# Feed-forward blocks in two halves, a third piece split by a transfer, and a first product in two matmuls

## The chip, the cores and the metric

The kernel runs on one core of one Trainium2 chip. Its time is the time of one execution on the device in microseconds (us). The kernel before took 2339.63 us, the median of three runs (2338.91 to 2342.20). The engines are called as in the profile: PE (matmuls; PEld its weight loads), DVE (VectorE), ACT (ScalarE), POOL (GpSimd) and SP, which here only issues transfers.

## The reference

One decoder layer on 256 tokens of 2048 features, all in float32. It runs a feed-forward part (FFN), a token mixer with two branches (sparse attention and a gated recurrence), and a second FFN, each followed by a layer norm:

```python
def swiglu(h, w_in, w_out):
    a, b = jnp.split(h @ w_in, 2, axis=-1)
    return (jax.nn.silu(a) * b) @ w_out

h = layer_norm(DN_ALPHA * h + 0.5 * swiglu(h, ffn1_w_in, ffn1_w_out), ln1_g, ln1_b)
...                       # projections, attention, recurrence, gates
h = layer_norm(DN_ALPHA * h + merged @ w_out, ln2_g, ln2_b)
h = layer_norm(DN_ALPHA * h + 0.5 * swiglu(h, ffn2_w_in, ffn2_w_out), ln3_g, ln3_b)
```

The inner width of each FFN is 5632: `w_in` is 2048 x 11264, `w_out` 5632 x 2048. Both FFNs run the same code, `ffn` (L1124), and the change lies there.

## The kernel before, in words

**Three products for one.** A float32 product is made of three matmuls in the format fp32r: every operand is split into a high part h (the value copied to fp32r by ACT) and a low part l (the value minus h, by DVE). `three` (L742) multiplies high by high, high by low and low by high into the same sums. The activations stand still in the array (128 x 128) and the weights stream past: 512 columns in `tokens` (L747), 256 in the forms below. So every weight has to be read from memory, copied by ACT (L275) and subtracted by DVE (L276).

**Blocks and chunks.** `w_in` of an FFN is cut into 22 blocks (`NBK`) of 256 columns of a and the 256 of b that belong to them. A block is four chunks of 512 rows. A chunk can go plainly, or by the scheme of seven products instead of eight (Strassen's in Winograd's form): the 2 x 2 quarters of the weights are added up on DVE (`operand`, L222: lines 230, 234, 237), and the seven products, of 256 columns each, are grouped into four *forms*: `p1q3`, `p2`, `q5p7` and `q4p6`. `p2` has one product, the other forms two, and each product is two units of three matmuls: 42 matmuls of 256 columns in a chunk. In blocks 6 to 21 (`FOUR`) all four chunks go by forms; these are the long blocks. The products add up in two banks `mm` (c) and two banks `bp` (e). `gate` (L1125) joins them at the block's end: ACT copies one quarter (L1132), DVE adds (L1133, L1134, L1135, L1139), ACT applies silu (L1140), DVE multiplies (L1145); some pieces later PE transposes the result (L1151) and it is split (L878, L879) into tiles g.

**Fills.** The second product, g @ `w_out`, is put among the blocks: `"o"` in a plan is a *piece* of `w_out`, 1024 columns wide in the tile and worth 12 matmuls of 512 columns. The blocks are grouped (`SEGS`: 2, then five times 4). While the blocks of one group run, the g of the group before is multiplied: each long block takes four pieces (k = 0, 2, 4, 6) for one quarter of the output columns; the sums then leave by ACT (L1174) and an adding transfer (L1175). With g as the group's number, blocks 6 to 9 work on g = 1 and blocks 10 to 21 on g = 2, 3 and 4.

**The plan.** `block_plan(FAST, 4, 3)` writes the order of a long block: three pieces, eight forms (two chunks), one piece, eight forms. PE, SP and POOL run in the order in which the program is written; ACT and DVE run in an order that a planner fixes before the run from its own costs.

**The supply of weights.** `Weights` walks one list of all pieces and forms. `unit` (L282) hands the next columns to PE; when it goes on to a new piece (`cur`), it loads up to `cur + AHEAD + LOADS` = 8 ahead (`load_to`, L216, on SP) and splits up to 4 ahead (`split_to`). Chunks of 1 MB are loaded into tiles `rf` (three of them in an FFN), pieces of 0.5 MB into `raw` (four), and split parts stand in five tiles `hl`.

**Pieces by transfer.** Some pieces take another way (`far`, `far_to`, L167): ACT writes minus the copy into a tile `wd` (L182), POOL issues a transfer that adds the piece from memory to it (L183), which gives l without DVE, and ACT writes h (L185). That is done `EARLY` = 12 pieces ahead, all four copies and both transfers at once; the raw tile is loaded four pieces before. The pieces k = 2 and k = 6 go this way, in g = 0 only for two quarters of the output: 34 pieces in an FFN.

Of the kernel before, what the change touches and what calls it, by code (L numbers as in the profile page):

```python
# [16 lines left out]
S = 256  # L17
# [43 lines left out]
HL_PITCH = 2112  # L61
BEGINS = (48, 16, 0)
AHEAD = 4
EARLY = 12
LOADS = 4
FORMS = ("p1q3", "p2", "q5p7", "q4p6")
PIECE = 1024
FAST = (0, 1, 2, 3)
# [31 lines left out]
FOUR = tuple(range(6, 22))  # L100


def layer_plans():
    three = (1, 2, 3)
    plans = [block_plan((), 0)] * 2
    plans += [block_plan((1, 3), 2, 0)] + [block_plan(three, 2, 2, late=False)] * 3
    for n in range(6, NBK):
        plans.append(block_plan(FAST if n in FOUR else three, 4, 3))
    return plans


# [26 lines left out]
class Weights:  # L138
# [8 lines left out]
    def __init__(self, nc, pool, pieces, on_piece):  # L147
        self.nc, self.pool, self.on_piece = nc, pool, on_piece
        self.fast_pool = self.third = None
        self.chunks = 0  # L150
        self.wide = None
        self.pieces = pieces
        self.raw = {}
        self.sums = {}
        self.hl = {}
        self.loaded = 0
        self.split = 0
        self.cur = -1
        self.limit = None
        self.cap = len(pieces)  # L160
        self.off = 0
        self.far = []
        self.apart = ()
        self.far_raw = {}
        self.far_loaded = self.far_split = 0

    def far_to(self, i):  # L167


        nc = self.nc  # L170
        while self.far_loaded < len(self.far) and self.far[self.far_loaded] <= i + LOADS:
            k = self.far[self.far_loaded]
            ap = self.pieces[k][0]
            t = self.far_raw[k] = self.pool.tile([P, PIECE], F32, name=f"raw{k}", tag="raw", bufs=RAW_BUFS)
            nc.sync.dma_start(t, ap)
            self.far_loaded += 1
        while self.far_split < len(self.far) and self.far[self.far_split] <= i:
            k = self.far[self.far_split]
            ap, t = self.pieces[k][0], self.far_raw.pop(k)
            h, l = ([self.wide() for _ in range(2)] for _ in range(2))  # L180
            for c in range(2):
                nc.scalar.activation(l[c], t[:, c * 512:(c + 1) * 512], AF.Copy, scale=-1.0)  # L182
                nc.gpsimd.dma_start(l[c], ap[:, c * 512:(c + 1) * 512], accum_op=OP.add)  # L183
            for c in range(2):
                nc.scalar.activation(h[c], t[:, c * 512:(c + 1) * 512], AF.Copy)  # L185
            self.hl[k] = (h, l)
            self.far_split += 1

    def key(self, i):
        ap, form = self.pieces[i]  # L190
# [91 lines left out]
    def unit(self, n):  # L282
        if self.cur < 0 or self.off == self.size(self.cur):
            self.hl.pop(self.cur, None)
            self.cur += 1
            self.off = 0
            self.far_to(self.cur + EARLY)
            self.load_to(self.cur + AHEAD + LOADS)
            self.split_to(self.limit or min(self.cur + AHEAD, self.cap))
            self.on_piece(self.size(self.cur) * (1 if self.pieces[self.cur][1] else 2))  # L290
        h, l = self.hl[self.cur]
        o = self.off
        self.off += n
        assert self.off <= self.size(self.cur)
        if self.cur in self.apart or self.cur in self.far:
            return h[o // 512], l[o // 512]
        return h[:, o:o + n], l[:, o:o + n]
# [70 lines left out]
def tile_layer(ctx, tc, x_fm, x_tm, pos, f1a, f1o, wA, wki, wB, wG, lru, wab, wrb, wo, f2a, f2o,  # L368
# [33 lines left out]

    bg = Background()

    pieces, far, apart = [], [], set()

    def keep_apart(n):
        apart.update(range(len(pieces) - n, len(pieces)))
# [6 lines left out]
    def block_pieces(ap, plan, fills=None, fo=None):  # L415
        chunk = {}
        for f, k in plan:
# [3 lines left out]
                plain([next(fills)])  # L421
            elif f == "o":
                g, nb, k = next(fills)
                if k in (2, 6) and (g or nb >= 2):
                    far.append(len(pieces))
                k += 2 * SEGS[g][0]
                pieces.append((fo[nb][:, k * 512:k * 512 + PIECE], None))
            else:
                if k not in chunk:
                    chunk[k] = ap[:, k * 2048:(k + 1) * 2048]  # L430
                pieces.append((chunk[k], f))
# [52 lines left out]
    keep_apart(WIDE)  # L484

    W = Weights(nc, pool, pieces, bg.paced)
    W.far, W.apart = far, apart
    W.across = {v.tensor.name for v in (wki, wB, lru)}
    W.wide = lambda: U("wd", F32R)
    W.fast_pool = ctx.enter_context(tc.tile_pool(name="f1", bufs=1))  # L490
# [251 lines left out]
    def three(ps, xh, xl, w, start, stop):  # L742
        T.matmul(ps, xh, w[0], start=start, stop=False)  # L743
        T.matmul(ps, xh, w[1], start=False, stop=False)  # L744
        T.matmul(ps, xl, w[0], start=False, stop=stop)  # L745

    def tokens(ps, x, t, w, start, stop):  # L747
        three(ps, x[:, 0, t * P:(t + 1) * P], x[:, 1, t * P:(t + 1) * P], w, start, stop)

    def eager(hs, ps):  # L750
# [28 lines left out]
    def blockF(x, forms, plan, fill):  # L779
# [14 lines left out]
        for i, (form, k) in enumerate(plan):  # L794
# [25 lines left out]

            def run(ps, ops, start, stop):
                for r in range(2):
                    three(ps, *ops[r], W.unit(S), start and r == 0, stop and r == 1)

            if form == "p1q3":
                run(p1, xop(0, 0), start[2], stop[2])
# [297 lines left out]
    def ffn(x, forms, ln):  # L1124
# [51 lines left out]

        for s, (b0, b1) in enumerate(SEGS):
            for n in range(b0, b1):
                c, e = blockF(x, forms, PLANS[n], fill)
                task = gate(c, e, g[s], 2 * (n - b0), LAG_T[n == NBK - 1], ("c", 0) in PLANS[n])  # L1180
                with tc.high_priority():
                    next(task)
                bg.add("gate", task)
        def back():
            for nb in range(4):
                for t in range(2):
# [509 lines left out]
```

## Time and profile before

| | before |
|---|---|
| median of three runs | 2339.63 us |
| profiled execution, its own time | 2340.27 us |
| its span | 2338.4 us |
| busy PE / DVE / ACT / POOL | 2312.5 / 2201.5 / 1560.0 / 263.4 us |
| one long block (of 32) | 31.4 us |
| moved by DMA | 546.97 MB, 234 GB/s on the mean |

A row of a timeline is: start, duration, engine, line, operation, the tile written and the tiles read, the shape, how many; in brackets the idle time before it and who ended it. `mm` and `bp` are banks of sums, `hl` split weights, `rf` and `raw` weights as loaded, `wd` the parts of a piece by transfer, `ws` the sums of quarters, `sh`/`sl` and `xs`/`hs` split activations, `z` the gate's tile, `g` its result. Matmuls are pipelined: a row's duration runs past the next one's start, so the distance of the starts is the pace. In the same way a DVE row's duration runs a little past the start of the next. In rows by stretch, the numbers are the length, then for each engine its busy time and its count of instructions, the granted clock as a share of full speed, the DMA engines' busy share, and GB/s.

### The profile page before, as it was taken

To read this page: it belongs to the slowest core of one execution; us is meant where nothing else is said; L and a number is where in the kernel's file an instruction comes from. 1 tells how busy PE (TensorE), PEld (TensorE's weight loads), DVE (VectorE), ACT (ScalarE), POOL (GpSimd) and SP (SyncE) were. 2 spreads that over 40 slices of the span, in tenths; PEclk is the share of its full clock that TensorE was granted. 3 is DMA by queue.
4 is the path that set the end of the run, shared out by engine and by line. 5 is a ranking of instruction groups with operands and counts; after the bars stand their busy time and mean duration, and the time that the engine had idled before them with its cause. 6 is when DMAs were issued, how large, how long until landed. Compare 5 with 4: busy or idle time off the path is not lost.

```text
span 2338.4 us, 40427 instructions
## 1 busy us (share of the span) xinstructions
PE 2312.5 (99%) x15430; PEld 2109.4 (90%) x15430; DVE 2201.5 (94%) x3196; ACT 1560.0 (67%) x2273; POOL 263.4 (11%) x368
## 2 busy tenths in 40 slices
PE   9999999999999999999999999999999999999998
PEld 7899999999988999888899998888889999999997
DVE  7999999999999999979887888998999999999997
ACT  7667777777757656556557785555667777777763
POOL 1101111111110000000100001100111111111111
PEclk9999999999999999999999999999999999999999
DMA  9878988888876556554675658655788888888875
GB/s 336 251 238 240 261 250 251 250 256 250 230 244 209 192 187 216 185 189 154 244 239 193 200 182 326 239 198 195 242 275 232 253 255 252 243 252 267 244 221 215
DMA packets 142178, 546.97 MB, mean 234 GB/s; under 512 B 16640, under 2 KB 17280, under 8 KB 117536
## 3 DMA queue, kind: packets, MB, share of 16 engines
q1 hardware_dynamic: 100800, 455.00, 55.1%
q0 software_dynamic: 41040, 89.27, 18.4%
q8 instruction: 120, 1.97, 0.3%
q14 instruction: 74, 0.61, 0.1%
q10 hardware_dynamic: 144, 0.13, 0.0%
HBM read 507.10 MB, written 37.22 MB: 233 GB/s over the span
## 4 chain that ended last, share of the span: by engine, by line
PE 66%; DVE 23%; issue 5%; DMA 3%; ACT 2%; POOL 0%; SPq 0%; ACTq 0%; DVEq 0%; POOLq 0%
PE mm L743 13%; PE mm L745 13%; PE mm L744 13%; DVE hl L276 13%; PE bp L744 5%; PE bp L745 5%; PE bp L743 4%; PE mm L1390 3%; PE mm L1389 3%; PE mm L1391 3%; DVE ws L230 2%; DVE rf L237 2%; DVE rf L234 2%; ACT hl L275 2%; DMA raw<-f1o 1%
## 5 line engine op out<-in xcount | busy, mean ns | idle before, releaser
L275 ACT ACTIVATE hl<-rf 128x1024 fp32r<-128x1024 f32 x573 | 511.3, 912 | 232.9 <-DVE rf L237 119.7
L276 DVE TENSOR_TENSOR hl<-rf,hl 128x1024 fp32r<-128x1024 f32 x573 | 596.9, 1047 | 8.2 <-ACT hl L275 3.8
L276 DVE TENSOR_TENSOR hl<-raw,hl 128x1024 fp32r<-128x1024 f32 (+3 forms) x402 | 474.2, 1196 | 62.2 <-ACT hl L275 61.4
L275 ACT ACTIVATE hl<-raw 128x1024 fp32r<-128x1024 f32 (+3 forms) x402 | 408.4, 1035 | 179.4 <-PE mm L745 82.8
L744 PE MATMUL bp<-hl,sh 128*128 128x256 f32 x1146 | 323.6, 282 | 10.1 <-DVE hl L276 10.1
L743 PE MATMUL bp<-hl,sh 128*128 128x256 f32 x1146 | 320.9, 280 | 0.0
L745 PE MATMUL bp<-hl,sl 128*128 128x256 f32 x1146 | 320.2, 279 | 0.0
L743 PE MATMUL mm<-hl,hs 128*128 128x512 f32 (+1 forms) x800 | 274.5, 343 | 1.6 <-DVE z L1139 0.7
L275 ACT ACTIVATE hl<-ws 128x1024 fp32r<-128x1024 f32 x191 | 202.0, 1058 | 102.7 <-DVE ws L230 71.5
L744 PE MATMUL mm<-hl,hs 128*128 128x512 f32 (+1 forms) x800 | 268.3, 335 | 0.0
L745 PE MATMUL mm<-hl,hs 128*128 128x512 f32 (+1 forms) x800 | 267.9, 335 | 0.1
L230 DVE TENSOR_TENSOR ws<-rf 128x1024 f32<-128x1024 f32 x191 | 233.8, 1224 | 5.4 <-DMA rf<-wrb 1.3
L276 DVE TENSOR_TENSOR hl<-ws,hl 128x1024 fp32r<-128x1024 f32 x191 | 234.2, 1226 | 1.8 <-ACT hl L275 1.7
L744 PEld LDWEIGHTS bp<-hl,sh 128*128 128x128 f32 x1146 | 215.4, 188 | 17.5 <-DVE hl L276 16.3
L745 PEld LDWEIGHTS bp<-hl,sl 128*128 128x128 f32 x1146 | 217.7, 190 | 0.0
L743 PEld LDWEIGHTS bp<-hl,sh 128*128 128x128 f32 x1146 | 215.4, 188 | 1.3
L1389 PE MATMUL mm<-hs,hl 128*128 128x256 f32 x640 | 178.3, 279 | 0.0
L1391 PE MATMUL mm<-hs,hl 128*128 128x256 f32 x640 | 177.8, 278 | 0.0
L1390 PE MATMUL mm<-hs,hl 128*128 128x256 f32 x640 | 177.7, 278 | 0.0
L743 PEld LDWEIGHTS mm<-hl,hs 128*128 128x128 f32 x800 | 150.4, 188 | 19.1 <-issue 2.6
L745 PEld LDWEIGHTS mm<-hl,hs 128*128 128x128 f32 x800 | 151.0, 189 | 16.7 <-DVE hs L937 0.5
L744 PEld LDWEIGHTS mm<-hl,hs 128*128 128x128 f32 x800 | 150.5, 188 | 14.3 <-DVE hl L276 0.2
(360 smaller groups left out, 5897.6 us busy)
## 6 DMA issues: line engine op xcount, KB each, us to landing
rf<-f1a SPq DMA_DIRECT2D x75, 1024.0 KB, 7.7
rf<-f2a SPq DMA_DIRECT2D x75, 1024.0 KB, 7.5
raw<-f1o SPq DMA_DIRECT2D x88, 512.0 KB, 6.6
raw<-f2o SPq DMA_DIRECT2D x88, 512.0 KB, 6.6
raw<-wB SPq DMA_DIRECT2D x80, 512.0 KB, 4.8
raw<-wG SPq DMA_DIRECT2D x54, 512.0 KB, 4.2
ya<-yd POOLq DMA_DIRECT2D x80, 256.0 KB, 7.4
rf<-wA SPq DMA_DIRECT2D x20, 1024.0 KB, 5.5
```

The costliest lines, as they stand in the source:

```text
L230: v.tensor_tensor(t, b[:, 0:4:3], b[:, 1:2].to_broadcast([P, 2, 2, 256]), op=OP.add)
L234: v.tensor_tensor(b[:, 1], t[:, 1], b[:, 0], op=OP.add)
L237: v.tensor_tensor(b[:, 0], b[:, 1], b[:, 2], op=OP.add)
L275: nc.scalar.activation(hp, src, AF.Copy)
L276: self.last = nc.vector.tensor_tensor(lp, src, hp, op=OP.subtract)
L743: T.matmul(ps, xh, w[0], start=start, stop=False)
L744: T.matmul(ps, xh, w[1], start=False, stop=False)
L745: T.matmul(ps, xl, w[0], start=False, stop=stop)
L1389: T.matmul(ps[:, :S], w[0], x[:, 0], start=first, stop=False)
L1390: T.matmul(ps[:, :S], w[0], x[:, 1], start=False, stop=False)
L1391: T.matmul(ps[:, :S], w[1], x[:, 0], start=False, stop=last)
```

## The change

Four things are changed, all for the two FFNs.

1. The order of a long block: `halves` writes two pieces, eight forms, two pieces, eight forms.
2. For g = 2, 3 and 4 (blocks 10 to 21) the piece k = 4 goes by transfer as well: 46 pieces in an FFN instead of 34. `EARLY` is 14 instead of 12, and the pieces of these groups are loaded eight pieces before their copies instead of four. The copies and transfers of such a piece are no longer written out at once: each new piece of the list takes one step (a low copy with its transfer, or a high copy), and what is left is done when the piece's turn comes.
3. In the long blocks the first unit of the first form behind a piece is written by `entry`: its first matmul, of 256 columns, becomes two of 128 columns. There are two such places in a block.
4. In the last block of an FFN the splitting ahead stops two pieces behind the block until the gate's first part is written.

```diff
-EARLY = 12
+EARLY = 14
 LOADS = 4
+FAR_LOADS = (4, 8)
...
+def halves(chunks):
+    forms = [(f, q) for q in chunks for f in FORMS]
+    n = len(forms) // 2
+    return 2 * [("o", 0)] + forms[:n] + 2 * [("o", 0)] + forms[n:]
...
     for n in range(6, NBK):
-        plans.append(block_plan(FAST if n in FOUR else three, 4, 3))
+        plans.append(halves(FAST) if n in FOUR else block_plan(three, 4, 3))
...
     def far_to(self, i):
...
-        while self.far_loaded < len(self.far) and self.far[self.far_loaded] <= i + LOADS:
+        while (self.far_loaded < len(self.far) and
+               self.far[self.far_loaded] <= i + FAR_LOADS[self.far[self.far_loaded] in self.soon]):
...
-            h, l = ([self.wide() for _ in range(2)] for _ in range(2))
-            for c in range(2):
-                nc.scalar.activation(l[c], t[:, c * 512:(c + 1) * 512], AF.Copy, scale=-1.0)
-                nc.gpsimd.dma_start(l[c], ap[:, c * 512:(c + 1) * 512], accum_op=OP.add)
-            for c in range(2):
-                nc.scalar.activation(h[c], t[:, c * 512:(c + 1) * 512], AF.Copy)
-            self.hl[k] = (h, l)
             self.far_split += 1
+            self.far_steps.append((k, self.far_copies(k, ap, t)))
+        if self.far_steps:
+            self.far_step()
+
+    def far_copies(self, k, ap, t):
+        nc = self.nc
+        h, l = [], []
+        for c in range(2):
+            l.append(self.wide())
+            nc.scalar.activation(l[c], t[:, c * 512:(c + 1) * 512], AF.Copy, scale=-1.0)
+            nc.gpsimd.dma_start(l[c], ap[:, c * 512:(c + 1) * 512], accum_op=OP.add)
+            yield
+        for c in range(2):
+            h.append(self.wide())
+            nc.scalar.activation(h[c], t[:, c * 512:(c + 1) * 512], AF.Copy)
+            if c == 0:
+                yield
+        self.hl[k] = (h, l)
+
+    def far_step(self):
+        if next(self.far_steps[0][1], self) is self:
+            self.far_steps.popleft()
...
             self.far_to(self.cur + EARLY)
+            while self.far_steps and self.far_steps[0][0] <= self.cur:
+                self.far_step()
...
-                if k in (2, 6) and (g or nb >= 2):
+                if k in (2, 6) and (g or nb >= 2) or k == 4 and g >= 2:
                     far.append(len(pieces))
+                    if g >= 2:
+                        soon.add(len(pieces))
...
+    after_wide = [False, False]
+
+    def entry(ps, xh, xl, w, start, stop):
+        n = w[0].shape[1] // 2
+        for c in range(2):
+            T.matmul(ps[:, c * n:(c + 1) * n], xh, w[0][:, c * n:(c + 1) * n], start=start and c == 0, stop=False)
+        T.matmul(ps, xh, w[1], start=False, stop=False)
+        T.matmul(ps, xl, w[0], start=False, stop=stop)
+
     def tokens(ps, x, t, w, start, stop):
+        after_wide[0] = after_wide[1] and w[0].shape[1] == 512
...
                 for r in range(2):
-                    three(ps, *ops[r], W.unit(S), start and r == 0, stop and r == 1)
+                    w = W.unit(S)
+                    (entry if after_wide[0] else three)(ps, *ops[r], w, start and r == 0, stop and r == 1)
+                    after_wide[0] = False
...
             for n in range(b0, b1):
+                after_wide[1] = n in FOUR
+                if n == NBK - 1:
+                    W.cap = W.cur + len(PLANS[n]) + 2
                 c, e = blockF(x, forms, PLANS[n], fill)
                 task = gate(c, e, g[s], 2 * (n - b0), LAG_T[n == NBK - 1], ("c", 0) in PLANS[n])
                 with tc.high_priority():
                     next(task)
+                W.cap = len(pieces)
                 bg.add("gate", task)
+        after_wide[:] = False, False
```

More of the change, by code (lines that the diff above doesn't have):

```diff
@@ L162, in __init__ @@
         self.far = []
+        self.soon = ()
         self.apart = ()
@@ L165, in __init__ @@
         self.far_loaded = self.far_split = 0
+        self.far_steps = deque()
     def far_to(self, i):
         nc = self.nc
-        while self.far_loaded < len(self.far) and self.far[self.far_loaded] <= i + LOADS:
+        while (self.far_loaded < len(self.far) and
+               self.far[self.far_loaded] <= i + FAR_LOADS[self.far[self.far_loaded] in self.soon]):
             k = self.far[self.far_loaded]
@@ L403, in tile_layer @@
     bg = Background()
-    pieces, far, apart = [], [], set()
+    pieces, far, apart, soon = [], [], set(), set()
     def keep_apart(n):
@@ L486, in tile_layer @@
     W = Weights(nc, pool, pieces, bg.paced)
-    W.far, W.apart = far, apart
+    W.far, W.apart, W.soon = far, apart, soon
     W.across = {v.tensor.name for v in (wki, wB, lru)}
```

## The prediction

> **What bounds the kernel now.** I read the page first, for the balance of the engines.
>
> ```profile
> PE 2312.5 (99%) x15430; PEld 2109.4 (90%) x15430; DVE 2201.5 (94%) x3196; ACT 1560.0 (67%) x2273; POOL 263.4 (11%) x368
> PE 66%; DVE 23%; issue 5%; DMA 3%; ACT 2%; POOL 0%; SPq 0%; ACTq 0%; DVEq 0%; POOLq 0%
> ```
>
> PE and DVE are both nearly full, so the share of the chain does not say which of them sets the pace. I therefore cut the two feed-forward stages into blocks, a block's end being the first read of its sums (L1132), and asked for busy times by stretch.
>
> ```profile
> core 0: us, PE busy (x) PEld busy (x) DVE busy (x) ACT busy (x) POOL busy (x), PEclk, DMA share, GB/s
> 347.55:378.96 31.41, 31.02 (x222) 28.92 (x221) 31.30 (x39) 22.91 (x33) 5.34 (x6) 1.00 0.86 254
> 190.40:284.75 94.35, 93.55 (x663) 87.35 (x662) 93.75 (x115) 68.42 (x97) 15.99 (x18) 1.00 0.87 251
> 284.75:662.47 377.72, 373.85 (x2643) 348.60 (x2642) 376.20 (x458) 270.55 (x377) 64.65 (x76) 1.00 0.85 249
> 1907.04:2284.40 377.36, 373.63 (x2644) 348.27 (x2643) 376.05 (x458) 270.31 (x378) 64.45 (x76) 1.00 0.83 248
> ```
>
> One block is 31.41 us; DVE works 31.30 of it. The two long rows are blocks 10 to 21 of each feed-forward: 24 blocks, 755.1 us. Blocks 7 to 9 (94.35 us for three) run the same way. The waits inside the first long row:
>
> ```profile
> PEld bp L744 <- DVE hl L276: 6.3, 12, 0.7
> PE bp L744 <- DVE hl L276: 3.9, 12, 0.5
> ```
>
> Twelve blocks, twelve waits of PE for a DVE subtraction; DVE waits for nobody there (no row with DVE on the left). So DVE sets the pace, and PE is close behind. How close is read from PE in order of time, in one block:
>
> ```profile
> 344.30 0.38 PE L744 MATMUL bp<-hl,sh 128*128 128x256 f32 x1 [0.27 <-DVE hl L276]
> 344.52 0.28 PE L745 MATMUL bp<-hl,sl 128*128 128x256 f32 x1
> 347.01 0.39 PE L743 MATMUL mm<-hl,g 128*128 128x512 f32 x1
> 355.19 0.28 PE L743 MATMUL bp<-hl,xs 128*128 128x256 f32 x1
> 358.72 0.60 PE L1151 MATMUL bp<-ident,z 128*128 128x128 f32 x4
> 359.08 0.37 PE L743 MATMUL mm<-hl,xs 128*128 128x256 f32 x1
> 359.28 0.28 PE L744 MATMUL mm<-hl,xs 128*128 128x256 f32 x1
> 365.30 0.39 PE L743 MATMUL mm<-wd,g 128*128 128x512 f32 x1
> ```
>
> Durations overlap, so starts are what counts. From 347.01 to 355.19 lie 36 matmuls of 512 columns, 0.2272 us each. From 355.19 to 358.72 lie 30 of 256 columns, 0.1177 each. Behind the four transposes, from 359.28 to 365.30, 53 of them take 0.1136 each, and behind the wait, from 344.52 to 347.01, 22 take 0.1132. There are two paces for the same matmul: slow behind the wide ones, until something breaks the row; fast after it.
>
> **The change, part by part.**
>
> *Third piece by transfer.* The low half of 24 more pieces (one in each of blocks 10 to 21) is made by an accumulating transfer. DVE loses one subtraction of a raw piece in each of these blocks.
>
> ```profile
> 345.46 2.35 DVE L276 TENSOR_TENSOR hl<-raw,hl 128x1024 fp32r<-128x1024 f32 x2
> 356.87 1.22 DVE L230 TENSOR_TENSOR ws<-rf 128x1024 f32<-128x1024 f32 x1
> 358.00 1.22 DVE L276 TENSOR_TENSOR hl<-rf,hl 128x1024 fp32r<-128x1024 f32 x1
> 363.87 1.22 DVE L230 TENSOR_TENSOR ws<-rf 128x1024 f32<-128x1024 f32 x1
> ```
>
> Such an operation lasts 1.22 but the next starts 1.13 later (358.00 less 356.87), so DVE falls from 31.30 to 30.17 us a block. Blocks 6 to 9 keep both subtractions: DVE still needs its 31.3, and I give them no gain.
>
> ACT gets four copies of 512 columns in place of one of 1024.
>
> ```profile
> 363.30 1.14 ACT L182 ACTIVATE wd<-raw 128x512 fp32r<-128x512 f32 x2
> 364.34 1.14 ACT L185 ACTIVATE wd<-raw 128x512 fp32r<-128x512 f32 x2
> 365.39 0.62 ACT L275 ACTIVATE hl<-rf 128x512 fp32r<-128x512 f32 x1
> L275 ACT ACTIVATE hl<-raw 128x1024 fp32r<-128x1024 f32 x385 | 399.6, 1056 | 177.9 <-PE mm L745 82.8 <-issue 22.1 <-PE bp L745 11.6
> ```
>
> The four take 2.09 us (363.30 to 365.39), the one 1.06: plus 1.0, to 24 of some 30.6 us. ACT's own idle time (8.5 us of the block now) covers it. Without that cover the subtractions behind it would be late by up to 1.0 us a block. The copies go out one per piece instead of four at once, so none of them holds the splits behind it for longer than about 0.5 us.
>
> POOL gets two issues more a block and the DMA engines 0.52 MB more.
>
> ```profile
> L183 POOL DMA_DIRECT2D wd<-f1o x68: 862/1226/1945, 88.2 to 624.3; - x68
> wd<-f1o POOLq DMA_DIRECT2D x68, 256.0 KB, 9.5
> q1 hardware_dynamic: 100800, 455.00, 55.1%
> q0 software_dynamic: 41040, 89.27, 18.4%
> ```
>
> POOL goes from 5.3 to 7.8 us a block, behind the same queue's stores of the sums (L1175), which nothing reads until the stage's end. Queue 0 costs 0.184 x 2338.4 / 89.27 = 4.8 us of all 16 engines per MB, so the block's DMA time goes from 0.86 x 31.4 = 27.0 to 29.5 us. That fits under 30.6, but barely; it is a rival below. The transfers are asked for 14 pieces ahead, half a block or more, against 9.5 us to land. The raw loads stay as many as they were on SP; for these pieces they stand four pieces earlier in its order. Up to four raw tiles exist, and I count three in use at once, so I take 0 for SP; a load that did block would delay the chunk loads behind it, which is the DMA rival again.
>
> ```profile
> 433.41 2.35 DVE L276 TENSOR_TENSOR hl<-rf,hl 128x1024 fp32r<-128x1024 f32 x2
> 439.92 2.35 DVE L276 TENSOR_TENSOR hl<-raw,hl 128x1024 fp32r<-128x1024 f32 x2
> 433.29 1.77 POOL L1175 DMA_DIRECT2D ya<-yd  x2 [4.27 <-ACT yd L1174]
> 434.38 2.48 POOL L183 DMA_DIRECT2D wd<-f1o  x2
> ```
>
> Under POOL's issues two subtractions take 2.35 us, and without them 2.35 too. So POOL's extra issues cost DVE nothing. [...]
>
> *Halves.* The order 3 + 8 + 1 + 8 of pieces and forms becomes 2 + 8 + 2 + 8. It adds no work. On PE the first forms come one wide piece, 12 x 0.227 = 2.7 us, earlier after a block's end. What must be ready then is the bank of their second product, which the gate of the block before has to have read:
>
> ```profile
> 347.55 0.36 ACT L1132 ACTIVATE z<-bp 128x256 f32<-128x256 f32 x1
> 348.87 0.41 DVE L1133 TENSOR_TENSOR z<-z,bp 128x256 f32<-128x256 f32 x1
> 350.33 0.42 DVE L1134 TENSOR_TENSOR z<-z,bp 128x256 f32<-128x256 f32 x1
> 351.26 0.69 DVE L1135 TENSOR_TENSOR z<-bp,z 128x512 f32<-128x512 f32 x1
> 352.46 1.02 DVE L1139 TENSOR_TENSOR z<-z,mm 128x512 f32<-128x512 f32 x2
> ```
>
> The block ended at 347.01; the first of the two L1139 is done about 353.05, 6.05 us later. PE now comes to that bank at 24 x 0.227 + 0.75 = 6.2 us, against 8.9 before. The margin falls from 2.8 to 0.15 us. With the order as it stands it costs 0; between these steps DVE has other work, and how that falls out in the new order the trace cannot show. Bounds: 0 if the order stays or is better, and 1.0 if the fillers become three of 1.13 instead of one of 1.13 and two of 0.6 (+1.06). I take 0.1 a block, nearest to the row. The buffering holds otherwise: a chunk costs DVE 6.3 (363.87 less 356.87, less two of 0.33 for the gate), so DVE has some 17.3 us in the first half (two chunks, one piece, 3.5 of the gate) and 12.7 in the second, against 15.3 of PE in each. The swing of 2 us fits into the four pieces that the five split buffers let it run ahead.
>
> *First product in two.* Two matmuls of 128 columns for one of 256, twice a block. Price, by the transposes: (359.08 - 358.72) / 4 = 0.09 each, so 0.18 for 0.118, +0.06. Lower bound 0; upper bound the 0.20 that PE took from 359.08 to 359.28, per product. [...] What it may bring: transposes of 128 columns put the row on the fast pace, and I take it that the pair does too. If so, 168 matmuls go at 0.1136 (19.08); if not, 42 before the transposes and 84 in the second half go at 0.1177, +0.52.
>
> *The cap* in the last block holds back two splits of the stage's tail until the gate's start: between 0 and 2 x 1.13 us a stage either way; the tail's pieces come after, I take 0.
>
> **Sum.** PE per block: 19.08 + 48 x 0.2272 (10.91) + transposes and the gap behind them 0.45 + 2 x 0.06 = 30.56; DVE 30.17 + 0.11 of gaps as now = 30.28. PE becomes the bound; with the 0.1 above 30.66, times 24 = 735.8 against 755.1: -19.3. The profiled execution took 2340.27 (span 2338.4 and 1.9 around it), 0.6 above the median of 2339.63; from its time 2321.0, and I state 2320.5 for a run like the median, 0.8% less. Its own range is 2315 to 2327 (0 to 0.3 a block for the gate).
>
> **Rivals.**
>
> *The pair doesn't change the pace.* For it: no row shows a pair behind wide matmuls; a wait does not always look like a transpose. Against: the break at 358.72. Then 31.08 + 0.1 a block: 748.3, -6.8: 2333.
>
> *The gate's chain takes the place of the wait.* For it: the margin of 0.15 us. Against: 12 blocks here share one order with 6.05. At the upper bound PE stands 0.9 us a block: 31.5, times 24 = +0.9, and blocks 6 to 9, whose PE has only some 0.5 to spare (the wait of 0.27 and the 0.22 to the next start), +0.4 each: about 2343, no change within what can be told. It begins to eat the gain when the first L1139 ends 6.2 us after the block's end.
>
> *The DMA engines become the bound: slower.* For it: 29.5 of 30.6 us are needed, yet in the block's middle they stand still, because chunk loads wait for their buffers:
>
> ```profile
> 416.00:421.40 5.40, 5.40 (x38) 4.97 (x37) 5.40 (x8) 3.52 (x5) 0.00 (x0) 1.00 0.24 61
> rf<-f1a SPq DMA_DIRECT2D x75, 1024.0 KB, 7.7
> ```
>
> That hole wastes 0.76 x 5.4 = 4.1 us. If it stays, a block needs 29.5 + 4.1 = 33.6: +2.1 x 24 = +51, 2391; with half of it left, 31.6 a block, 2343. It decides from 1.9 us of hole on (31.4 - 29.5). Against: the new transfers are spread over the block, and a chunk load has more time than 7.7 us until its tile's turn, three tiles and 30 us for four chunks.
>
> [...]
>
> *The change doesn't move the bound*, because DVE's order leaves it idle where it was busy: 2340.
>
> **How the numbers follow.** Forecast 0.57; the pair without effect 0.17; the gate's chain 0.09; no move 0.05; DMA 0.09; POOL 0.03. A measurement here can tell about 0.2% (4.7 us) from no change. Faster takes the forecast, the pair's rival and a little of the gate's (partial stalls): 0.75. Same: the rest of the gate's, no move, and the mildest DMA: 0.14. Slower: 0.11. The range goes from 2314 (no stall at all and a tail gain of 1 us) to 2341: it takes in the first two cases and most of the unchanged ones, and leaves out some 0.18.
>
> **What would show it.** Right: blocks 10 to 21 at 30.5 to 30.8 us with DVE at 30.2, its share under 99%; waits of PE for L276 gone; 256-column starts 0.1136 apart right behind the pair; blocks 7 to 9 still 31.4. Wrong: 0.1177 behind the pair; PE waiting for L1139 at the second product; DVE waiting for a load of rf; subtractions longer than 1.22 under POOL. The forecast as a whole is wrong if the 24 blocks stay above 31.2.

## The result, and the profile after

The changed kernel takes 2361.34 us (median of four runs, 2360.25 to 2362.05) against 2339.45 for the kernel before on the same chip: a ratio of 1.0089, 95% interval 1.0076 to 1.0101. It is slower by 0.9%, where 0.8% faster was forecast. A range up to 2341 does not hold it.

The page of the changed kernel: busy time of the engines, and the chain that ended last.

```profile
PE 2316.8 (98%) x15494; PEld 2111.5 (89%) x15494; DVE 2183.5 (93%) x3172; ACT 1590.5 (67%) x2345; POOL 306.0 (13%) x416
PE 72%; DVE 20%; issue 3%; DMA 3%; ACT 2%; SPq 0%; POOL 0%; ACTq 0%; DVEq 0%; POOLq 0%
```

DVE's busy time fell by 18 us, and the time still went up. Where, is read by cutting both traces at the same points. Here a block ends with the start of its last matmul of 256 columns; the two feed-forwards are added up.

| stretch | before | after | difference |
|---|---|---|---|
| up to the end of block 2 | 79.5 | 78.7 | -0.8 |
| blocks 3 to 5 | 160.9 | 169.1 | +8.2 |
| blocks 6 to 9 | 250.2 | 255.8 | +5.6 |
| blocks 10 to 21 | 754.2 | 762.8 | +8.6 |
| the mixer, to the second block 2 | 1038.5 | 1038.5 | 0.0 |
| the rest | 55.1 | 55.4 | +0.3 |

So the stretch that was to give 19.3 us costs 8.6, and 13.8 more come from blocks in which no time was forecast to move. By stretch, blocks 10 to 21 of the changed kernel (columns as before):

```profile
290.46:670.96 380.50, 373.86 (x2665) 349.14 (x2664) 366.53 (x445) 283.54 (x409) 84.08 (x98) 1.00 0.90 261
1922.88:2305.18 382.30, 375.01 (x2665) 350.00 (x2664) 366.63 (x445) 283.49 (x408) 84.09 (x98) 0.99 0.90 260
```

DVE works 30.5 us a block there (366.53 / 12), 0.4 above the 30.17 of the forecast, but a block takes 31.7 to 31.9. Now DVE stands still, which it did not do before. The waits in the first of these stretches:

```profile
ACT z L1181 <- DVE z L1180: 25.2, 12, 3.6
DVE hl L301 <- ACT hl L300: 11.5, 23, 1.4
PE mm L772 <- DVE z L1180: 6.4, 7, 1.8
```

Two things are seen in order of time, in the block whose sums are read at 321.70. First the gate on DVE, then PE at the first matmul that needs the bank:

```profile
324.08 0.41 DVE L1174 TENSOR_TENSOR z<-z,bp 128x256 f32<-128x256 f32 x1
324.42 1.22 DVE L301 TENSOR_TENSOR hl<-ws,hl 128x1024 fp32r<-128x1024 f32 x1
325.55 0.41 DVE L1175 TENSOR_TENSOR z<-z,bp 128x256 f32<-128x256 f32 x1
325.88 1.22 DVE L301 TENSOR_TENSOR hl<-rf,hl 128x1024 fp32r<-128x1024 f32 x1
327.02 0.68 DVE L1176 TENSOR_TENSOR z<-bp,z 128x512 f32<-128x512 f32 x1
327.62 1.21 DVE L255 TENSOR_TENSOR ws<-rf 128x1024 f32<-128x1024 f32 x1
328.75 1.01 DVE L1180 TENSOR_TENSOR z<-z,mm 128x512 f32<-128x512 f32 x2
```

```profile
329.58 0.36 PE L772 MATMUL mm<-hl,sh 128*128 128x256 f32 x1 [1.66 <-DVE z L1180]
```

Three long operations stand between the gate's additions. Second, ACT and DVE in the second half of the same block:

```profile
342.90 1.14 ACT L200 ACTIVATE wd<-raw 128x512 fp32r<-128x512 f32 x2
343.94 0.62 ACT L205 ACTIVATE wd<-raw 128x512 fp32r<-128x512 f32 x1
344.46 1.06 ACT L1215 ACTIVATE yd<-mm 128x512 f32<-128x512 f32 x2
345.41 0.62 ACT L205 ACTIVATE wd<-raw 128x512 fp32r<-128x512 f32 x1
345.93 1.15 ACT L200 ACTIVATE wd<-raw 128x512 fp32r<-128x512 f32 x2
346.98 0.62 ACT L300 ACTIVATE hl<-rf 128x512 fp32r<-128x512 f32 x1
```

```profile
347.63 0.69 DVE L301 TENSOR_TENSOR hl<-rf,hl 128x512 fp32r<-128x512 f32 x1 [1.07 <-ACT hl L300]
348.58 1.22 DVE L301 TENSOR_TENSOR hl<-ws,hl 128x1024 fp32r<-128x1024 f32 x1 [0.26 <-ACT hl L300]
```

Six copies for pieces by transfer and two for the sums stand in one row, and the copy that DVE needs next stands behind them: DVE loses 1.33 us.

In blocks 2 to 5 a copy on ACT stands at its head and waits for a raw load, and DVE waits for ACT:

```profile
98.57 0.63 ACT L200 ACTIVATE wd<-raw 128x512 fp32r<-128x512 f32 x1 [3.17 <-DMA raw<-f1o]
1710.87 1.15 ACT L200 ACTIVATE wd<-raw 128x512 fp32r<-128x512 f32 x2 [4.46 <-DMA raw<-f2o]
```

```profile
100.18 1.22 DVE L301 TENSOR_TENSOR hl<-rf,hl 128x1024 fp32r<-128x1024 f32 x1 [2.60 <-ACT hl L300]
```

### The profile page after: what moved, and what is told of

It reads as the page before. It is cut to its first block, busy times and chain, and to the rows that moved or that the text cites. A ratio compares the mean times of both kernels' runs of the same rounds, so it can differ in the third digit from the quotient of the medians.

```text
span 2360.3 us, 40722 instructions
## 1 busy us (share of the span) xinstructions
PE 2316.8 (98%) x15494; PEld 2111.5 (89%) x15494; DVE 2183.5 (93%) x3172; ACT 1590.5 (67%) x2345; POOL 306.0 (13%) x416
## 4 chain that ended last, share of the span: by engine, by line
PE 72%; DVE 20%; issue 3%; DMA 3%; ACT 2%; SPq 0%; POOL 0%; ACTq 0%; DVEq 0%; POOLq 0%
PE mm L772 15%; PE mm L773 15%; PE mm L774 15%; DVE hl L301 10%; PE bp L772 5%; PE bp L773 5%; PE bp L774 5%; PE mm L1436 3%; PE mm L1438 3%; PE mm L1437 3%; DVE ws L255 2%; ACT hl L300 2%; DVE rf L262 1%; DVE rf L259 1%; DVE z L1180 1%
## 5 line engine op out<-in xcount | busy, mean ns | idle before, releaser
L300 ACT ACTIVATE hl<-rf 128x1024 fp32r<-128x1024 f32 x573 | 509.9, 912 | 251.7 <-DVE rf L262 152.8
L301 DVE TENSOR_TENSOR hl<-raw,hl 128x1024 fp32r<-128x1024 f32 (+2 forms) x378 | 446.7, 1192 | 65.4 <-ACT hl L300 63.3
L300 ACT ACTIVATE hl<-raw 128x1024 fp32r<-128x1024 f32 (+2 forms) x378 | 386.8, 1034 | 177.0 <-PE mm L774 82.5
```

The costliest lines, as they stand in the source:

```text
L300: nc.scalar.activation(hp, src, AF.Copy)
L301: self.last = nc.vector.tensor_tensor(lp, src, hp, op=OP.subtract)
```

## The experiments

Theory 1: the gate's chain is late for the bank that PE reaches earlier. Theory 2: the new handling of the early pieces makes ACT wait for loads. The rival: the third piece itself costs, by its copies or its transfers. A third theory was formed on the way. In the kernels below the line numbers shift by a few. The stretches in this table are cut as above, both feed-forwards added up; each ratio is to the runs of the kernel before on the same chip.

| kernel | blocks 3-5 | 6-9 | 10-21 | median, us | ratio to before (95%) |
|---|---|---|---|---|---|
| before | 160.9 | 250.2 | 754.2 | 2340.9 | |
| changed | 169.1 | 255.8 | 762.8 | 2361.3 | 1.0076 to 1.0101 |
| order undone | 168.9 | 254.1 | 740.3 | 2339.7 | 0.9986 to 1.0005 |
| early pieces as before | 160.3 | 255.4 | 758.8 | 2352.5 | 1.0030 to 1.0060 |
| gate together | 169.6 | 254.8 | 763.5 | 2364.2 | 1.0082 to 1.0112 |
| copies spread | 168.4 | 257.2 | 802.7 | 2401.1 | 1.0234 to 1.0277 |
| gate together, copies spread | 168.1 | 254.4 | 742.1 | 2340.4 | 0.9989 to 1.0008 |
| halves alone | 161.3 | 252.6 | 753.3 | 2343.3 | 1.0003 to 1.0022 |
| third piece from block 6 on | 162.2 | 248.0 | 739.2 | 2324.6 | 0.9915 to 0.9944 |

**The order undone.** The rest of the change stays.

```diff
-        plans.append(halves(FAST) if n in FOUR else block_plan(three, 4, 3))
+        plans.append(block_plan(FAST if n in FOUR else three, 4, 3))
```

> The changed kernel with the halves undone (order 3 + 8 + 1 + 8 again); third piece by transfer, pair and cap kept. Theory 1 (the gate's chain: with two pieces in front PE comes to the bank of the second product before the two reads of it by L1180 are done; 24 blocks cost 7.7 us more than before instead of 19 less): PE's waits for L1180 at the second product go, blocks 10 to 21 take 30.9 to 31.1 us instead of 31.8, the three 34 us blocks with the low clock go; 2361 less 20 to 24: 2337 to 2341. Theory 2 (the early blocks 2 to 5, where ScalarE stands before a far piece's copy whose raw load has not come): those blocks stay 28 us, so nothing below 2335. Rival (the third piece itself costs, by its copies on ACT or its transfers): blocks stay at 31.5 to 31.8, 2355 to 2361.

Measured: 2339.72 us. PE's wait for L1180 is gone from blocks 10 to 21, which take 30.8 us each: 22.5 us less than in the changed kernel and 13.9 less than before. The rival falls: the third piece with its copies and transfers is in this kernel and the blocks are faster than before. The kernel is no faster than before because blocks 3 to 9 lose 11.9 us.

**The early pieces as before.** The pieces of the first two groups are loaded 16 ahead and copied all at once 12 ahead, as in the kernel before (16, not the 14 that the expectation names); the halves stay.

```diff
-               self.far[self.far_loaded] <= i + FAR_LOADS[self.far[self.far_loaded] in self.soon]):
+               self.far[self.far_loaded] <= i + (8 if self.far[self.far_loaded] in self.soon else 2)):
...
-        while self.far_split < len(self.far) and self.far[self.far_split] <= i:
+        while (self.far_split < len(self.far) and
+               self.far[self.far_split] <= i - (0 if self.far[self.far_split] in self.soon else 2)):
...
+            while k not in self.soon and self.far_steps:
+                self.far_step()
```

> The changed kernel, but the far pieces that it shares with the kernel before (first two groups) are fetched and copied as before: load 14 pieces ahead, all four copies at once 12 ahead; the pieces of the last groups keep the new way. Theory 2: blocks 2 to 5 go from 28.3 back to 26.6 us in both feed-forwards, some 9 us in all, and ScalarE's waits for raw there go: 2350 to 2354. Theory 1: the long blocks keep their waits for L1180, so not below 2348. If the early blocks were slow for the gate's or the mixer's reasons: 2360 to 2362.

Measured: 2352.48 us, 8.9 less than the changed kernel; blocks 3 to 5 are back at 160.3. Theory 2 holds for these blocks, not for blocks 6 to 9.

**The gate together.** Same work; between long blocks the splits of the third and fourth form of the next block are ordered behind the gate's last addition on DVE.

```diff
-                    V.tensor_tensor(zt, zt, c[t][:, :w], op=OP.add)
+                    W.hold = V.tensor_tensor(zt, zt, c[t][:, :w], op=OP.add).ins
...
+                W.held = (W.cur + 5, W.cur + 6) if n in FOUR and n + 1 in FOUR else ()
...
+            wait = self.tc.issue_after(self.hold) if self.split in self.held else nullcontext()
```

> The changed kernel, with one thing: between blocks of the long kind the splits of the third and fourth form of the next block's first chunk are ordered on DVE behind the gate's last L1180. So DVE does the gate's five additions one behind the other, with the same work and the same order everywhere else. Theory 1: the first L1180 is done some 4 to 5 us after the block's end instead of 7 to 8, PE comes at 6.2: waits go, long blocks 30.8 to 31.0 us: 24 x 0.9 = 21 less, 2338 to 2342. If it were not the fillers but the two-piece lead in any order, or the third piece: 2355 or more. If holding the two splits makes PE wait for them instead: waits for L301 of 0.5 to 1 us a block, 2345 to 2355.

Measured: 2364.19 us, no gain. The first stretch of blocks 10 to 21 and its waits:

```profile
292.19:674.00 381.81, 374.93 (x2665) 347.06 (x2664) 369.30 (x445) 278.71 (x409) 84.22 (x98) 1.00 0.92 261
```

```profile
ACT z L1187 <- DVE z L1186: 42.0, 12, 4.7
DVE hl L305 <- ACT hl L304: 9.3, 22, 0.7
PE bp L779 <- DVE hl L305: 3.5, 12, 0.5
```

The first of the two additions now starts 3.7 us after the block's end, and PE does not wait for it. But DVE still waits for ACT, and PE now pays at L305, the splits. Theory 1 alone falls. From this came theory 3: ACT's row of copies, which takes from DVE what the third piece gave it.

**Both of these orders.** The gate together, and the early pieces as before.

> Both: the gate's additions together on DVE, and the far pieces of the first two groups handled as in the kernel before. If theories 1 and 2 hold and add: 2361 - 21 - 9 = 2331, range 2327 to 2335, faster than the kernel before by 0.3 to 0.5%. If they overlap or only one holds: 2338 to 2352.

Measured: 2357.91 us (ratio 1.0068, 1.0051 to 1.0084), above both ranges: 6.3 less than the gate together, which is theory 2's part; the long blocks stay at 763.2.

**The copies spread.** Each copy for a new piece is ordered on ACT behind the copy of the split written just before it.

```diff
+            with self.tc.issue_after(self.copied) if k in self.soon else nullcontext():
+                nc.scalar.activation(l[c], t[:, c * 512:(c + 1) * 512], AF.Copy, scale=-1.0)
...
+            with self.tc.issue_after(self.copied) if k in self.soon else nullcontext():
+                nc.scalar.activation(h[c], t[:, c * 512:(c + 1) * 512], AF.Copy)
...
-                nc.scalar.activation(hp, src, AF.Copy)
+                self.copied = nc.scalar.activation(hp, src, AF.Copy).ins
```

> The changed kernel, with one thing: each of ScalarE's copies for the new far pieces (last groups) is ordered behind ScalarE's copy of the split that is written just before it in the program, so six or eight of them no longer stand in one row in front of the splits in the middle of a block. Same work, same order on PE. Theory 3 (formed from the run with the gate's additions together, in which PE's waits only moved to L305 and the long blocks stayed at 31.8: DVE works 30.5 us a block and then waits 1.0 to 1.15 us a block for ScalarE's copies, 25.7 us in the 24 blocks; PE's wait for L1180 is only where DVE's lateness is paid): DVE's waits for ACT go, long blocks 30.6 to 30.9: 2361 less 20 to 26: 2335 to 2341. Theory 1 (three long fillers between the gate's additions make PE wait, whatever ScalarE does): PE keeps waiting 0.5 to 1.8 for L1180 in most blocks, 2353 to 2361.

Measured: 2401.06 us, far outside both. The row of copies is gone, but the planner answered with another order on DVE: three long operations between the gate's additions in every block, not in some. The stretch and its waits:

```profile
292.29:691.18 398.89, 378.37 (x2662) 353.71 (x2661) 367.98 (x443) 288.21 (x413) 84.19 (x100) 0.98 0.89 248
```

```profile
ACT z L1185 <- DVE z L1184: 41.2, 12, 3.7
DVE hl L304 <- ACT hl L303: 26.8, 34, 1.7
PE mm L776 <- DVE z L1184: 20.5, 12, 1.9
```

It is a ring. PE waits 1.7 us in each block for the gate; ACT, in order, stands 3.4 us before silu; the copies behind silu are late; DVE waits 2.2 us a block for them. So theory 3 alone falls as well, and theory 1's mechanism is seen at full size. It is not a clean test of one cause, since the order on both engines moved.

**The gate together and the copies spread.** Both edits.

> The changed kernel with both orders: ScalarE's copies spread and the gate's five additions together on DVE. If only theory 3 is right: as with the copies spread alone, within 4 us. If both have a part: 2335 to 2340 here and 2345 to 2355 with the copies spread alone. If neither (the two pieces in front of the forms cost by something else, or the third piece by transfer as such): 2355 or more in both.

Measured: 2340.39 us, 21 less than the changed kernel. Blocks 10 to 21 of the two feed-forwards, and the gate in one block:

```profile
292.75:661.43 368.68, 368.07 (x2657) 345.24 (x2656) 365.53 (x442) 285.58 (x413) 84.22 (x100) 1.00 0.96 268
1914.90:2283.73 368.83, 368.04 (x2656) 345.04 (x2655) 365.67 (x442) 285.64 (x412) 84.20 (x100) 1.00 0.96 267
```

```profile
354.74 0.42 DVE L1183 TENSOR_TENSOR z<-z,bp 128x256 f32<-128x256 f32 x1
355.20 0.42 DVE L1184 TENSOR_TENSOR z<-z,bp 128x256 f32<-128x256 f32 x1
355.65 0.69 DVE L1185 TENSOR_TENSOR z<-bp,z 128x512 f32<-128x512 f32 x1
356.38 1.02 DVE L1189 TENSOR_TENSOR z<-z,mm 128x512 f32<-128x512 f32 x2
```

From block 11 on every block takes 30.78 to 30.86 us. In the first of the two stretches PE is busy for all but 0.6 of 368.68 and waits once. So the lateness had two sources, as expected if both have a part; only the 2345 to 2355 expected of the copies alone did not come (2401). With the gate's order mended alone a block takes 31.8 us, with the copies' alone 33.4, with both 30.8. By their busy times PE (30.8) and DVE (30.5) have only 0.3 us a block to spare for each other, so one source is enough to hold the blocks up.

**The order undone, and the early pieces as before.** The first two edits.

> The changed kernel with the halves undone and the far pieces of the first two groups handled as in the kernel before. The order of before alone gave 2339.7 with long blocks of 30.8 instead of 31.45 before, and blocks 2 to 9 some 14 us slower than before over both feed-forwards. Theory 2 (those early pieces' loads and copies): they come back, by the 9 us that this was worth with the halves: 2339.7 less 9 to 13: 2327 to 2331, faster than before. If the early loss comes from elsewhere (the new transfers' queue, the plan of blocks 6 to 9): 2336 to 2340.

Measured: 2330.94 us (ratio 0.9960, 0.9946 to 0.9974), 8.8 less than with the order undone alone: theory 2 has its price twice. Blocks 3 to 5 take 160.5, blocks 10 to 21 741.5. Blocks 6 to 9 stay at 253.5, 3.3 above before.

**The halves alone.** The kernel before with the one line of the plan.

> The kernel before with the halves alone; no third piece by transfer, no pair, no cap, no new handling. DVE sets the pace here at 31.3 to 31.4 us a block and did not wait for ScalarE. Theory 1 (the two-piece lead makes PE wait for L1139): 0.5 to 1.0 us a block, 2350 to 2363. Theory 3 (ScalarE's bunched copies, which are not here): 2338 to 2344, no change.

Measured: 2343.34 us, 0.13% over before. DVE sets the pace as before: it works 31.28 us of a block's 31.39 (375.32 and 376.68, each by 12). No wait of PE is long enough to be listed:

```profile
284.67:661.35 376.68, 376.68 (x2641) 351.69 (x2640) 375.32 (x457) 270.04 (x376) 64.09 (x76) 1.00 0.84 249
```

There the first addition of the second product starts 3.9 us after the block's end, in the kernel before 5.5. So the shorter lead does not cost by itself. What costs is the lead together with the order on DVE that came with the rest of the change.

**All three mended.** The gate together, the copies spread, the early pieces as before.

> The changed kernel, halves and pair and third piece kept, with the gate's additions together on DVE, ScalarE's new copies spread, and the far pieces of the first two groups handled as in the kernel before. If the three causes found so far add: 2340.4 less the 8.8 to 8.9 us that the last was worth twice: 2331 to 2332, range 2328 to 2335; faster than before by 0.3 to 0.5%. If the early pieces cost only through the orders already mended: 2339 to 2341.

Measured: 2335.24 us (ratio 0.9973, 0.9963 to 0.9983): 5.1 less than without the last edit, not 8.8. Blocks 3 to 5 take 163.1 here, 160.5 with the order undone. The halves as such do not make these 2.6 us: with the early pieces as before and the halves they take 160.3. They take 163.5 when the gate's order joins, and 160.2 in a later version with all three mended, a third piece from block 6 on and no pair. What makes the difference was not singled out.

**The early copies spread too.** As the kernel with gate together and copies spread, but every piece by transfer is tied; loads and distances stay as in the change.

```diff
-            with self.tc.issue_after(self.copied) if k in self.soon else nullcontext():
+            with self.tc.issue_after(self.copied) if self.copied else nullcontext():
```

> The changed kernel with the gate's additions together and ScalarE's copies spread for all far pieces, those of the first two groups too, which keep their new distances (load 18 pieces ahead, copies from 14 ahead, one a piece). Theory 2a (ScalarE's planned order pulls those copies in front of splits, where they stand and wait for a raw load of 128 x 1024 that has not landed): blocks 2 to 5 come back, as with the old handling, 2331 to 2334. Theory 2b (the new distance itself: the loads stand earlier in SP's order and take a raw buffer or the DMA engines when the chunks need them): no gain, 2338 to 2341.

Measured: 2335.51 us (ratio 0.9978, 0.9967 to 0.9988), the same as with the old handling, and 1.5 above the range of theory 2a. ACT's waits for a raw load in blocks 2 to 5 are gone, and blocks 3 to 5 take 163.1 instead of 168.1. So it is the place of the copy in ACT's order, not the earlier load, that cost (theory 2a).

**Without the pair.** The version with the order undone and the early pieces as before, `entry` switched off.

```diff
-                after_wide[1] = n in FOUR
+                after_wide[1] = False
```

> The version that gave 2330.9 (halves undone, old handling of the early far pieces) without the pair of 128 columns. Forecast on record: with the pair 168 matmuls at 0.1136, without it 126 of them at 0.1177 (+0.52 a block), and the two pairs cost 0.1 each as measured: 0.3 a block for 24 blocks, and part of it in blocks 6 to 9 where DVE sets the pace: 7 to 9 us slower, 2338 to 2340. If the pair does not change the pace, or only moves the wait: 2329 to 2332, or a little faster by the price of the pairs (2326).

Measured: 2330.15 us (ratio 0.9953, 0.9938 to 0.9968): no difference, where 7 to 9 us were expected. Long blocks take 30.90 instead of 30.78, but blocks 6 to 9, where DVE sets the pace, take 251.7 instead of 253.5.

**The third piece from block 6 on.** All three mended, and g = 1 gets the third piece and the new handling as well.

```diff
-                if k in (2, 6) and (g or nb >= 2) or k == 4 and g >= 2:
+                if k in (2, 6) and (g or nb >= 2) or k == 4 and g:
...
-                    if g >= 2:
+                    if g:
```

> As the version with all three mended, and the third piece by transfer already in blocks 6 to 9 too, with the new way of loading and copying for their far pieces. DVE sets the pace of blocks 6 to 9 now (31.4 to 32.7 us); with 1.13 less it would be PE at 30.8: 4 x 0.6 to 1.0 in each feed-forward, 4 to 8 us less than the version with all three mended: 2323 to 2328. If the load and copies of those pieces come too early, as in blocks 2 to 5: 2331 to 2340.

Measured: 2324.61 us, 0.7% faster than before and 1.6% faster than the change. Blocks 6 to 9 take 248.0 instead of 255.1, and PE waits for nobody in blocks 10 to 21 of either feed-forward:

```profile
284.30:653.00 368.70, 368.70 (x2662) 345.93 (x2661) 365.65 (x443) 285.42 (x412) 84.21 (x100) 1.00 0.96 269
1901.33:2270.12 368.79, 368.79 (x2662) 346.02 (x2661) 365.98 (x443) 285.53 (x412) 84.15 (x100) 1.00 0.96 268
```

**The same without the pair.** Here PE alone sets the pace in all the long blocks.

> The version that gave 2324.6 (all three mended, third piece from block 6 on) without the pair of 128 columns. There PE sets the pace in blocks 6 to 21 and waits for nobody, so what the pair does must show in full: by the paces in the traces, a pair and the gap behind it take 0.34 us where one matmul took 0.12, and the 82 behind it go at 0.1136 instead of 0.1178: 0.07 us gained by the pair in front of the short row (42) and 0.25 in front of the long one (84), 0.32 a block, times 32 blocks: 10 us slower without it, 2332 to 2337. If the pair brings nothing, as the null result in the order of before suggests: 2323 to 2327.

Measured: 2333.82 us, 9.2 more (ratio to before 0.9973, 0.9963 to 0.9983). The stretch is 373.04 instead of 368.70, 0.36 us a block:

```profile
283.87:656.91 373.04, 373.04 (x2637) 350.53 (x2636) 365.14 (x443) 285.36 (x413) 84.21 (x100) 1.00 0.96 266
```

The pair does what it says, where PE sets the pace. By the starts of the matmuls in like blocks, the second half's row takes 9.52 us with it and 9.78 without, the row in front of the transposes 4.88 and 4.95. A short row hardly repays the pair.

**The same with the order undone.** Copies spread, three pieces in front, and the gate left with its long operations between.

> The version that gave 2324.6, but with the halves undone (3 + 8 + 1 + 8) and the gate's additions left where the planned order puts them, three long fillers between them. Copies spread, pair kept. Theory 1 by its margin: PE comes to the bank of the second product 8.9 us after a block's end instead of 6.2, and the first L1187 is done by 8.0, so no waits for it although the order on DVE is the one that cost 60 us with the halves: long blocks 30.8, 2321 to 2327. If the fillers or the spread copies cost by themselves: long blocks over 31.5, 2345 or more.

Measured: 2326.36 us (ratio 0.9939, 0.9926 to 0.9951). The first addition starts 6.3 to 7.9 us after a block's end here, about as late as in the version that took 2401 (7.4). It is done by 8.5, and in these blocks PE never waits for it. The one wait of PE in this stretch is for the landing of a piece's transfer:

```profile
282.88:651.38 368.50, 367.79 (x2658) 343.50 (x2657) 363.68 (x443) 282.44 (x410) 83.60 (x98) 1.00 0.91 267
PE mm L780 <- DMA wd<-f1o: 0.6, 1, 0.6
```

So it is the margin: a gate that is late by this much costs when PE reaches the bank at 6.2 us, and not at 8.9. And the halves bring nothing that can be told, 2324.6 against 2326.4.

## Why the prediction was wrong, point by point

**The gate's chain: the step that failed.** It was costed at 0.1 us a block, "nearest to the row", with bounds of 0 and 1.0 "if the fillers become three of 1.13". Three long ones they became for six of the 24 gates, and two for the others: the first addition starts 5.6 to 7.5 us after the block's end (before 5.5), and PE waits 0 to 1.79 us for it. In the 24 blocks these waits add up to 13.2 us, 0.55 a block where 0.1 was in the sum. The forecast left a margin of 0.15 us and took DVE's order of before for granted, though the same edit took an operation out of that order. The bound was too small too. With three long fillers 4.67 us lie between the gate's first addition and this one instead of 3.6, which is the bound's 1.06; but DVE also came late to the first, 2.5 to 2.8 us after the block's end instead of 1.9 to 2.0. And in three of the blocks the granted clock was 0.50 for 3.41 us behind the wait (last section), 4.9 us in all, which the sum did not have. A margin of that size should have been costed at its upper end, with the chance to match; 0.09 was given to it.

**ACT: the second step that failed.** "ACT's own idle time (8.5 us of the block now) covers it" and "none of them holds the splits behind it for longer than about 0.5 us". The idle time was there, ACT is busy for 23.6 of 31.7 us; the place was not. The program writes one copy per piece, but ACT's order is the planner's, which drew them together. DVE lost 11.5 us in twelve blocks by it, about 1.0 a block of the 1.13 it was given. The text itself had named the price without the cover: up to 1.0 a block.

These two make the loss in blocks 10 to 21: with both orders mended they take 742.1 us against 762.8, and 735.8 was forecast. Of the 6.3 left, 3.4 is PE's own pace (30.80 a block, with 30.66 in the sum), and 2.8 lies in the two blocks 10, which follow blocks that DVE still holds up.

**The third piece.** Right: DVE works 30.5 us a block, and once nothing stalls it PE sets the pace. DMA, POOL and SP were right too: the DMA share is 0.96 in the fastest version, 29.5 us of a block as forecast, and PE waits for nobody there. With the order of before it waits for a piece's transfer to land up to three times in twelve blocks, for at most 0.7 us. In blocks 10 to 21 of the changed kernel a subtraction of 1024 columns takes 1.22 us under POOL's issues and 1.22 without them. So nothing here shows DVE held up by POOL, to which 0.03 was given.

**The pair: right in what it does, its price too low by 0.1 a block.** The forecast was a gain of 0.52 for a price of 0.12, net 0.40; 0.36 was measured. But the floor with it is 30.79 a block, not 30.56. PE in one block of the version that took 2324.61, first in the row behind the transposes, then at a pair:

```profile
388.57 0.29 PE L785 MATMUL bp<-hl,sh 128*128 128x256 f32 x1
389.99 0.33 PE L785 MATMUL mm<-hl,xs 128*128 128x256 f32 x1
390.16 0.28 PE L786 MATMUL mm<-hl,xs 128*128 128x256 f32 x1
396.77 0.33 PE L793 MATMUL bp<-hl,xs 128*128 128x128 f32 x2
396.94 0.33 PE L794 MATMUL bp<-hl,xs 128*128 128x256 f32 x1
397.11 0.28 PE L795 MATMUL bp<-hl,xs 128*128 128x256 f32 x1
```

The pair's two starts take 0.17 us and the next start comes 0.17 behind it, 0.34 for three starts, where two at 0.1136 take 0.23: 0.11 each, not 0.06. The transposes give this as well, once the late start behind them is counted in: (359.28 - 358.72) / 5 = 0.112, three are 0.336; the prediction left that start out. The rest of the 0.23 a block (30.79 less 30.56) is in the row behind the transposes, which the forecast put at 0.1136 throughout. Here it falls back to the slow pace: the 12 starts from 388.57 to 389.99 are 0.118 apart. The next start comes 0.17 later, and the pace recovers: in the block before, behind the same start (359.36), the six starts from 359.84 to 360.52 are 0.113 apart. The row's 42 matmuls take 5.02 us (median of blocks 11 to 21), where 4.86 was in the sum. Why it falls back is open.

**The halves: "It adds no work."** For PE they do. Where PE waits for nobody, a block without the pair takes 31.16 us with the halves (in the version of 2333.82) and 30.90 with the order of before (2330.15). The two rows around the transposes make this: 42 and 42 matmuls take 10.03 us, 30 and 54 take 9.76. With the pair it is 30.79 (2324.61) against 30.65 in the blocks without a wait (2326.36). So part of what the pair gains is what the halves had cost.

**Blocks 6 to 9: "I give them no gain".** No loss was forecast either, and they lost 5.6 us. DVE keeps both subtractions there and has next to nothing to spare (before, it works 93.75 of the 94.35 us of blocks 7 to 9). The halves alone cost 2.4 (252.6), and the pair 1.8 with the order of before (253.5 with it, 251.7 without). All the versions with the pair and two pieces by transfer there stay 3.3 to 7.0 above before, and the rest was not taken apart; with the third piece there as well they are 2.2 below.

**The cap** was not run alone. 0 was forecast, and the rest of the table, in which the tails lie, moved by 0.3.

**Blocks 3 to 5 were not costed at all.** The change of `EARLY` and of the steps reaches them, and they cost 8.2 us by copies that stand in ACT's order in front of their load. The forecast had looked at the loads in SP's order only.

**The sum.** From 2320.5 to 2361.3 are 40.8 us; by the profiles 41.2: 27.9 in blocks 10 to 21 (8.6 and 19.3), 13.8 in blocks 3 to 9, less 0.5 elsewhere. The rival "the gate's chain takes the place of the wait" was the right one in its place and its deciding point (6.2 us), and its 2343 was 18.3 too low: by 8.2 in blocks 3 to 5, 2.4 in blocks 6 to 9 (it had 3.2 there) and 7.7 in blocks 10 to 21 (it had 0.9), 4.9 of these by the lowered clock.

## What to carry to other kernels

When two engines are both nearly full, taking work off one can be worth nothing while a stall on the way is larger than the slack between them (here 0.55 us a block at PE, against 0.3): look at what the change does to the order on each engine, not only to its sum. Where a planner orders an engine, writing operations apart does not keep them apart; tie them to what they must not pass. And a margin of a tenth of a microsecond at a bank (0.15 us here, and waits of up to 1.79) is no margin: it is to be priced as lost.

## What was not expected of the hardware

Behind three of PE's waits in the changed kernel, of 1.78 to 1.79 us, the granted clock was 0.50 for 3.41 us; behind three others, of 1.46, 1.66 and 1.78, it stayed at 1.00. The changed kernel, just behind a wait of 1.79 us that ended at 582.50:

```profile
583.00:585.00 2.00, 2.00 (x12) 2.00 (x11) 2.00 (x4) 1.08 (x3) 0.00 (x0) 0.52 0.99 400
```

The three blocks took 34.3 us instead of 32.7, 4.9 us more in all. In the version with the copies spread every long block has a wait of 1.69 to 1.90; twelve of 24 take 32.6 to 32.7 us and the other twelve 34.2 to 34.5. Two stretches of it behind equal waits (1.69 us, ended at 431.58 and at 464.20):

```profile
433.60:435.60 2.00, 2.00 (x20) 2.00 (x19) 1.93 (x3) 1.70 (x2) 0.00 (x0) 1.00 0.99 397
466.00:468.00 2.00, 2.00 (x12) 2.00 (x11) 1.14 (x3) 1.09 (x2) 0.00 (x0) 0.50 0.99 406
464.74:468.15 3.41, 3.41 (x18) 3.41 (x17) 2.51 (x5) 2.06 (x3) 0.00 (x0) 0.50 0.98 390
```

The drops of this trace lie on a grid. Each lasts 3.41 us, as the third row has it, and in the first feed-forward they begin at 300.90, 464.74, 498.87, 533.01 and 567.14: the later ones 48, 58, 68 and 78 times 3.413 us behind the first. Of the two waits, the first is cut by a point of this grid (430.61), the second lies between two points (461.33 and 464.74). Of the 24 waits in blocks 10 to 21, five are cut by a point, and no drop followed on any of them; on twelve of the 19 others a drop followed at the next point. What sets the other seven apart is not shown. The drops of the changed kernel lie on such a grid too: they begin at 583.08, 1962.07 and 2091.77, the later two 404 and 442 times 3.4133 us behind the first.

The twelve longer blocks stand 3.4 to 3.7 us above the 30.8 of the version with both orders mended, the twelve others 1.8 to 1.9.
